# A two-layer hybrid backbone: attention values as one chain over all query blocks

## The chip, the core and the metric

The kernel runs on one core of a Trainium2 chip. The metric is the device time of one execution in microseconds (us), as the median of several runs. A core has five engines that each work through their own instructions in order and wait for one another by semaphores: PE (TensorE: matrix multiplications, and transposes as multiplications with an identity), DVE (VectorE), ACT (ScalarE), POOL (GpSimd) and SP, which here only issues DMAs.

## What is computed

Two layers over 1024 latent and 256 context tokens. Each layer projects a normalised and modulated stream into the inputs of three branches (windowed attention, a convolution with a LayerNorm, a bidirectional linear recurrence called LRU), gates and merges them, and normalises again. The change touches the values of attention, the two einsums with `p_loc` and `p_ctx`:

```python
def window_attention(q, k, v, k_ctx, v_ctx, sink):
    ...
    p = jax.nn.softmax(jnp.concatenate([s_loc, s_ctx, s_sink], -1), axis=-1)
    p_loc = p[..., :3 * BLOCK].astype(v.dtype)
    p_ctx = p[..., 3 * BLOCK:3 * BLOCK + C].astype(v.dtype)
    out = jnp.einsum('bnhgqj,bnjhd->bnqhgd', p_loc, vb) + jnp.einsum('bnhgqc,bchd->bnqhgd', p_ctx, v_ctx)
```

A query block is 128 queries of one key/value head with its four query heads. Its keys are two context blocks and up to three neighbouring latent blocks of 128: two to five key blocks. Layer 0 has 20 query blocks with 84 key blocks in all, layer 1 (latent queries only) 16 with 76.

## The kernel before

Every large product is made in single-precision parts: an operand is split into a rounded part on ACT (`whi`, `ph`, `hlhi`) and a remainder on DVE (`wlo`, `pl`, `hllo`), and the product is three (or, for the values, two) matmuls into one PSUM tile.

Each layer has two phases. In phase 1 nine generators run side by side: `lru`, `att_values`, `att_scores`, `lru_in`, `lru_out`, `att_proj`, `att_out`, `conv` and `gates`. A generator emits some instructions and yields the engine on which its next step waits. A `Driver` keeps a reckoning of each engine's time, picks by readiness and priority (`PRIO`) which generator goes on, and a scheduler behind it orders the instructions of each engine once more. So the order on an engine is fixed before the program runs, and every move of one generator moves the others. `gates` (24 weight columns with 2 or 3 products each) and the gating products of `lru_out`, `conv` and `att_out` are the reserve that fills PE while other generators wait.

Three pools are booked by counters: `sl` (10 wide SBUF slots), `hl_` (14 half slots of 128x512, for almost every generator) and `pl_` (4 PSUM tiles of one bank, shared by products, turned keys and value sums).

`att_values` takes one query block at a time. For each key block j it turns four 128x128 pieces of the probabilities into a PSUM tile `pt` (four transposes on PE), splits it into `ph` (ACT) and `pl` (DVE), and one step later lets the function `values` add two matmuls to the block's sum `yp`. After the last key block come its joining: `yt` (two copies on ACT, then two additions on DVE) and a DMA of the 128x512 result. Before each block it takes four half slots and one PSUM tile, and gives them back behind the joining. With T for the four transposes and V for the two matmuls, a block reads T0 T1 V0 T2 V1 ... V(last), joining.

The convolution's LayerNorm stands beside it: for a token tile, a sum matmul `ps<-sm` on PE, four centring instructions on DVE (`ab`, `acc2`, `acc`), four squares `sq` on ACT, a second sum matmul. It needs six half slots (`LH`). There are three such tiles in layer 0 and two in layer 1.

Of the kernel before, what the change touches and what calls it, by code (L numbers as in the profile page):

```python
# [9 lines left out]
F32R = mybir.dt.float32r  # L10
# [179 lines left out]
def kernel(  # L190
# [8 lines left out]
    pe, act, dve = Meter(nc.tensor, pe_cost), Meter(nc.scalar, act_cost), Meter(nc.vector, dve_cost)  # L199
# [19 lines left out]
    def f32(ap):  # L219
        return ap.bitcast(F32)  # L220

    def psum(n=512, name="ps"):
        return PM.tile([128, n], F32, tag="mm", name=name, bufs=4)
# [6 lines left out]
    ident = K.tile([128, 128], F32, tag="ident", name="ident")  # L230
# [121 lines left out]
    def split(src, hi, lo):  # L352
        act.activation(out=hi, in_=src, func=AF.Copy)
        dve.tensor_tensor(out=lo, in0=src, in1=f32(hi), op=ALU.subtract)
# [167 lines left out]
    def both(*conds):  # L522
        return lambda: all(c() for c in conds)

    def phase1(l, R, RH):
# [5 lines left out]
        sl, hl_, pl_ = Pool_(NS), Pool_(NHF), Pool_(4)  # L531
# [5 lines left out]
        def half(name, dt=F32):  # L537
            return RH.tile([128, 512], dt, tag="h", name=name, bufs=NHF)
# [323 lines left out]
        at = dict(proj=[], ready=[], done={0: 0, 1: 0}, issued=0, ks={}, vs={})  # L862
        tiles0 = 2 if last else 0
        blocks = [(kv, t) for kv in range(2) for t in range(tiles0, 10)]
# [159 lines left out]
                at["ready"].append((kv, tl, keys, pv, drv_.t["dve"]))  # L1024

        def att_values():
            for i in range(len(blocks)):
                yield ("pe", both(lambda: len(at["ready"]) > i, hl_.room(4)))
                kv, tl, keys, pv, tm = at["ready"][i]
                vs = at["vs"][kv]  # L1030
                hl_.take(4)
                yield ("pe", tm, lambda: pl_.used <= 2)
                pl_.take()
                yp = psum(name="yp")
                pend = None

                def values(j, ph, pl, stop):
                    pe.matmul(out=yp, lhsT=vs[:, keys[j], :], rhs=ph, start=(j == 0), stop=False)
                    pe.matmul(out=yp, lhsT=vs[:, keys[j], :], rhs=pl, start=False, stop=stop)

                for j in range(len(keys)):
                    pt = psum(name="pt")
                    for hh in range(4):
                        pe.transpose(pt[:, hh * 128:hh * 128 + 128], pv[hh][:, j * 128:j * 128 + 128], ident)
                    ph, pl = half("ph", F32R), half("pl", F32R)
                    split(pt, ph, pl)
                    yield "pe"
                    if pend:
                        values(*pend, False)
                        yield "pe"  # L1050
                    pend = (j, ph, pl)
                values(*pend, True)
                sl.give(2)
                yield "act"
                yt = half("yt")
                ypv = yp.rearrange("p (a e q) -> p a e q", e=2, q=128)
                ytv, yo = (yt[:, o:o + 256].rearrange("p (a q) -> p a q", q=128) for o in (0, 256))
                act.activation(out=ytv[0:64], in_=ypv[64:128, :, 0, :], func=AF.Copy)
                act.activation(out=ytv[64:128], in_=ypv[0:64, :, 1, :], func=AF.Copy)
                yield "dve"  # L1060
                for e in range(2):
                    r = slice(64 * e, 64 * e + 64)
                    dve.tensor_tensor(out=yo[r], in0=ypv[r, :, e, :], in1=ytv[r], op=ALU.add)
                sp.dma_start(out=ya_d[kv * 256:kv * 256 + 256, tl * 128:tl * 128 + 128].rearrange("(c p) t -> p c t", p=128),
                             in_=yo)
                pl_.give()
                hl_.give(4)
                at["done"][kv] += 1
                if at["done"][kv] == per_kv:
                    sl.give()  # L1070

        def att_out():
            for j in range(4):
                yield ("pe", lambda: at["done"][j // 2] == per_kv)

                def get(nt):
                    y = half("ya")
                    sp.dma_start(out=y[:, 0:nt[2]], in_=ya_d[j * 128:j * 128 + 128, nt[1]:nt[1] + nt[2]])
                    return y[:, 0:nt[2]]

                yield from gating(0, j, get, 1.0)
# [15 lines left out]
        def gates():  # L1097
# [27 lines left out]
            assert not todo  # L1125

        drv_.run([lru(), att_values(), att_scores(), lru_in(), lru_out(), att_proj(), att_out(), conv(), gates()], PRIO[l])
        assert wlive[0] == 0 and sl.used == 0 and hl_.used == 0 and pl_.used == 0

# [274 lines left out]
    for l in range(DEPTH):  # L1404
        drv_.phase = 2 * l
        phase1(l, RS, RH)
        ss.close()

        def open_b():
            hs.close()  # L1410
            return open_pool(f"b{l}", 1 - l)

        drv_.phase = 2 * l + 1
        phase2(l, lambda: open_pool(f"a{l}", l), open_b, lambda: open_pool(f"c{l}", l))
        if l < DEPTH - 1:
            hs, RH = open_pool(f"h{l + 1}", l)
            ss, RS = open_pool(f"s{l + 1}", 1 - l)
# [46 lines left out]
```

## Time and profile before

| | |
|---|---|
| median of 3 runs | 2307.63 us (2306.44 to 2307.89) |
| the profiled execution | 2307.8 us, span 2306.0 us |
| granted TensorE clock, mean | 0.99 |
| busy share of the span | PE 98%, weight loads 81%, DVE 73%, ACT 44% |

The span reaches from the first to the last instruction; 1.8 us lie outside it. Attention's values run in layer 0 from 460 to 925 us and in layer 1 from 1665 to 2062 us.

### The profile page before, as it was taken

The page shows a single profiled execution, that of the slowest core. Times are in us where ns is not written, and L with a number is a line of the kernel's source. Part 1 is how long each engine was busy: PE and PEld are TensorE (multiplying, and loading weights), DVE is VectorE, ACT ScalarE, POOL GpSimd, SP SyncE. Part 2 cuts the span into 40 slices and gives each one's busy share as a digit, 9 for nine tenths or more (in the row PEclk, how much of TensorE's full clock was granted, in tenths as well). Part 3 has the DMA queues.
Part 4 walks back from the last instruction along what each step waited for, and adds up shares of the span by engine and source line. Part 5 has one row for each costly group of instructions (what it writes and reads, how often), then busy time and mean ns, then how long its engine had stood idle before and what let it go on. Part 6 is the DMA issues. An engine that isn't in the chain of part 4 may idle for free.

```text
span 2306.0 us, 29961 instructions
## 1 busy us (share of the span) xinstructions
PE 2249.3 (98%) x11344; PEld 1871.8 (81%) x11344; DVE 1678.9 (73%) x2453; ACT 1003.4 (44%) x1642; POOL 86.7 (4%) x140
## 2 busy tenths in 40 slices
PE   7999999999999999999999999999999999999998
PEld 2888888888888887888888788888888878778886
DVE  5579967868959875545678749869778787655667
ACT  4555563245444575422122644565344456542110
POOL 1000000000000111000001100000000011000002
PEclk8999999999999999999999999999999999999999
DMA  7223323433334232655562222233423334347532
GB/s 276 76 73 101 115 73 126 142 112 108 108 101 138 80 117 87 203 167 168 151 206 74 94 66 67 80 92 128 142 90 97 89 122 131 111 136 227 160 128 92
DMA packets 270946, 279.90 MB, mean 121 GB/s; under 512 B 19769, under 2 KB 199889, under 8 KB 270801
## 3 DMA queue, kind: packets, MB, share of 16 engines
q1 hardware_dynamic: 242288, 226.06, 31.4%
q10 hardware_dynamic: 28512, 51.92, 6.4%
q8 instruction: 89, 1.46, 0.3%
q14 instruction: 57, 0.46, 0.1%
HBM read 203.04 MB, written 74.88 MB: 121 GB/s over the span
## 4 chain that ended last, share of the span: by engine, by line
PE 88%; DVE 5%; ACT 2%; DMA 2%; issue 2%; SPq 0%; POOLq 0%; POOL 0%; ACTq 0%; DVEq 0%
PE ps L73 82%; PE yp L73 3%; PE pt L73 2%; PE pa L73 1%; DVE acc L73 1%; DMA raw<-in_w_ada_dram 1%; DVE P L73 1%; DVE pl L73 1%; DVE wlo L73 1%; DMA yst<-yd 1%; ACT whi L73 0%; DMA qd<-qd 0%; DVE xp L73 0%; PE p L73 0%; ACT hf L73 0%
## 5 line engine op out<-in xcount | busy, mean ns | idle before, releaser
L73 PE MATMUL ps<-hlhi,whi 128*128 128x512 f32 x1728 | 681.9, 395 | 2.2 <-DVE gs L73 1.0
L73 PE MATMUL ps<-hllo,whi 128*128 128x512 f32 x1728 | 678.4, 393 | 0.0
L73 PE MATMUL ps<-hlhi,wlo 128*128 128x512 f32 x1728 | 676.8, 392 | 0.0
L73 PEld LDWEIGHTS ps<-hlhi,wlo 128*128 128x128 f32 x1728 | 325.8, 189 | 67.5 <-issue 0.4
L73 PEld LDWEIGHTS ps<-hlhi,whi 128*128 128x128 f32 x1728 | 326.5, 189 | 66.5 <-DVE pl L73 2.2
L73 PEld LDWEIGHTS ps<-hllo,whi 128*128 128x128 f32 x1728 | 326.2, 189 | 62.7 <-issue 0.7
L73 DVE SCALAR_TENSOR_TENSOR acc<-u,cwt,acc 128x1296 f32<-128x1296 f32 (+1 forms) x240 | 342.3, 1426 | 2.2
L73 ACT ACTIVATE whi<-raw 128x1024 fp32r<-128x1024 f32 x180 | 190.0, 1058 | 334.1 <-PE ps L73 299.9
L73 DVE TENSOR_TENSOR wlo<-raw,whi 128x1024 fp32r<-128x1024 f32 x180 | 220.4, 1225 | 95.1 <-ACT whi L73 91.5
L73 PE MATMUL ps<-yy,whi 128*128 128x512 f32 (+1 forms) x960 | 271.6, 368 | 2.8 <-DVE m L73 2.8
L73 PEld LDWEIGHTS ps<-yy,whi 128*128 128x128 f32 x960 | 173.7, 188 | 33.5 <-DVE m L73 3.2
L73 PE MATMUL ps<-yy,wlo 128*128 128x512 f32 (+1 forms) x480 | 176.6, 368 | 0.0
L73 ACT ACTIVATE ph<-pt 128x512 fp32r<-128x512 f32 x160 | 93.9, 591 | 130.5 <-PE pt L73 125.1
L73 DVE TENSOR_TENSOR pl<-pt,ph 128x512 fp32r<-128x512 f32 x160 | 108.9, 685 | 50.8 <-ACT ph L73 49.4
L73 PE MATMUL ps<-hchi,whi 128*128 128x256 f32 x480 | 135.6, 283 | 1.3 <-ACT whi L73 0.5
L73 ACT ACTIVATE P<-P,nm 128x640 f32<-128x640 f32 (+1 forms) x128 | 101.9, 798 | 79.7 <-DVE nm L73 79.6
L73 PE MATMUL ps<-hchi,wlo 128*128 128x256 f32 x480 | 135.3, 282 | 1.0 <-DVE wlo L73 1.0
L73 PE MATMUL ps<-hclo,whi 128*128 128x256 f32 x480 | 134.6, 281 | 0.0
L73 DVE CUSTOM_DVE_ANT_0 P<-ps,m_mid,nsink 128x640 f32<-128x640 f32 (+1 forms) x112 | 93.0, 859 | 42.3 <-PE ps L73 40.8
L73 ACT ACTIVATE tg<-ps,drv 128x512 f32<-128x512 f32 (+1 forms) x120 | 76.4, 637 | 68.3 <-PE ps L73 67.7
L73 PEld LDWEIGHTS ps<-yy,wlo 128*128 128x128 f32 x480 | 90.5, 188 | 15.0
L73 PE MATMUL pt<-ident,P 128*128 128x128 f32 x640 | 97.2, 274 | 3.1 <-DVE pl L73 1.4
(205 smaller groups left out, 3396.1 us busy)
## 6 DMA issues: line engine op xcount, KB each, us to landing
raw<-in_w_in_dram SPq DMA_DIRECT2D x60, 512.0 KB
raw<-in_w_ada_dram SPq DMA_DIRECT2D x48, 512.0 KB
raw<-in_w_gate_dram SPq DMA_DIRECT2D x48, 512.0 KB
th<-tg ACTq DMA_DIRECT2D x96, 256.0 KB
thl<-th SPq DMA_DIRECT2D x96, 256.0 KB
yd<-gs ACTq DMA_DIRECT2D x48, 256.0 KB
yst<-yd SPq DMA_DIRECT2D x48, 256.0 KB
raw<-in_w_branch_dram SPq DMA_DIRECT2D x24, 512.0 KB
```

The costliest lines, as they stand in the source:

```text
L73: return f(*a, **k)
```

## The change

`att_values` holds the pending key block in a list that outlives the query block. The turning of the next block's first key block is emitted ahead of the last `values` of the block before, and the joining comes behind that. When the next block's probabilities are not there yet, the pending step is flushed first. The PSUM tile for `yp` is taken at a block's first `values`, no longer ahead of its first turning. The four half slots are taken once, when the generator starts (that is at the start of phase 1), and given back at its end; each block takes one more for `yt`.

```diff
--- before.py
+++ after.py
@@ -1024,32 +1024,20 @@
                 at["ready"].append((kv, tl, keys, pv, drv_.t["dve"]))
 
         def att_values():
-            for i in range(len(blocks)):
-                yield ("pe", both(lambda: len(at["ready"]) > i, hl_.room(4)))
-                kv, tl, keys, pv, tm = at["ready"][i]
-                vs = at["vs"][kv]
-                hl_.take(4)
-                yield ("pe", tm, lambda: pl_.used <= 2)
-                pl_.take()
-                yp = psum(name="yp")
-                pend = None
-
-                def values(j, ph, pl, stop):
-                    pe.matmul(out=yp, lhsT=vs[:, keys[j], :], rhs=ph, start=(j == 0), stop=False)
-                    pe.matmul(out=yp, lhsT=vs[:, keys[j], :], rhs=pl, start=False, stop=stop)
-
-                for j in range(len(keys)):
-                    pt = psum(name="pt")
-                    for hh in range(4):
-                        pe.transpose(pt[:, hh * 128:hh * 128 + 128], pv[hh][:, j * 128:j * 128 + 128], ident)
-                    ph, pl = half("ph", F32R), half("pl", F32R)
-                    split(pt, ph, pl)
+
+            pend = []
+
+            def values():
+                q, j, ph, pl = pend.pop()
+                if j == 0:
+                    pl_.take()
+                    q["yp"] = psum(name="yp")
+                keys, yp, vs = q["keys"], q["yp"], at["vs"][q["kv"]]
+                pe.matmul(out=yp, lhsT=vs[:, keys[j], :], rhs=ph, start=(j == 0), stop=False)
+                pe.matmul(out=yp, lhsT=vs[:, keys[j], :], rhs=pl, start=False, stop=(j == len(keys) - 1))
+                if j < len(keys) - 1:
                     yield "pe"
-                    if pend:
-                        values(*pend, False)
-                        yield "pe"
-                    pend = (j, ph, pl)
-                values(*pend, True)
+                    return
                 sl.give(2)
                 yield "act"
                 yt = half("yt")
@@ -1061,13 +1049,36 @@
                 for e in range(2):
                     r = slice(64 * e, 64 * e + 64)
                     dve.tensor_tensor(out=yo[r], in0=ypv[r, :, e, :], in1=ytv[r], op=ALU.add)
+                kv, tl = q["kv"], q["tl"]
                 sp.dma_start(out=ya_d[kv * 256:kv * 256 + 256, tl * 128:tl * 128 + 128].rearrange("(c p) t -> p c t", p=128),
                              in_=yo)
                 pl_.give()
-                hl_.give(4)
+                hl_.give(1)
                 at["done"][kv] += 1
                 if at["done"][kv] == per_kv:
                     sl.give()
+
+            hl_.take(4)
+            for i in range(len(blocks)):
+                if pend and len(at["ready"]) <= i:
+                    yield from values()
+                yield ("pe", both(lambda: len(at["ready"]) > i, hl_.room()))
+                kv, tl, keys, pv, tm = at["ready"][i]
+                q = dict(kv=kv, tl=tl, keys=keys)
+                hl_.take(1)
+                yield ("pe", tm, lambda: pl_.used <= 2)
+                for j in range(len(keys)):
+                    pt = psum(name="pt")
+                    for hh in range(4):
+                        pe.transpose(pt[:, hh * 128:hh * 128 + 128], pv[hh][:, j * 128:j * 128 + 128], ident)
+                    ph, pl = half("ph", F32R), half("pl", F32R)
+                    split(pt, ph, pl)
+                    yield "pe"
+                    if pend:
+                        yield from values()
+                    pend.append((q, j, ph, pl))
+            yield from values()
+            hl_.give(4)
 
         def att_out():
             for j in range(4):
```

The number and the shapes of the instructions stay as they were. The order changes from the LRU stretch of layer 0 on, on every engine.

**The end of layer 1's attention, on PE and ACT.** In these rows `pt` are the turnings, `yp` the value sums, `ph` and `pl` the two parts, `P` the probabilities. On PE before, from the first turning of the last block but one (`pt_17719`) on:

```order
L73 MATMUL pt_17719<-ident_81,P_17307 128x128 x2
L73 MATMUL pt_17719<-ident_81,P_17349 128x128 x2
L73 MATMUL yp_17640<-pl_17694,vs_16094 128x512
L73 MATMUL pt_17728<-ident_81,P_17307 128x128 x2
L73 MATMUL pt_17728<-ident_81,P_17349 128x128 x2
L73 MATMUL yp_17640<-ph_17704,vs_16094 128x512
L73 MATMUL yp_17640<-pl_17705,vs_16094 128x512
L73 MATMUL yp_17718<-ph_17724,vs_16094 128x512
L73 MATMUL pt_17739<-ident_81,P_17307 128x128 x2
L73 MATMUL pt_17739<-ident_81,P_17349 128x128 x2
L73 MATMUL yp_17718<-pl_17725,vs_16094 128x512
```

After, the corresponding rows, from `pt_17710` on:

```order
L73 MATMUL pt_17710<-ident_81,P_17354 128x128 x2
L73 MATMUL pt_17710<-ident_81,P_17411 128x128 x2
L73 MATMUL yp_17674<-pl_17694,vs_16138 128x512
L73 MATMUL yp_17674<-ph_17704,vs_16138 128x512
L73 MATMUL pt_17727<-ident_81,P_17354 128x128 x2
L73 MATMUL pt_17727<-ident_81,P_17411 128x128 x2
L73 MATMUL yp_17674<-pl_17705,vs_16138 128x512
L73 MATMUL yp_17736<-ph_17715,vs_16138 128x512
L73 MATMUL yp_17736<-pl_17716,vs_16138 128x512
L73 MATMUL pt_17739<-ident_81,P_17354 128x128 x2
L73 MATMUL pt_17739<-ident_81,P_17411 128x128 x2
L73 MATMUL yp_17736<-ph_17732,vs_16138 128x512
```

Before, two turnings of the new block stand ahead of the old block's last `values` (`ph_17704`, `pl_17705`), and the new block's first `values` (`ph_17724`) follow at once; now one turning stands ahead of them, and a second is not far ahead. On ACT, in the same place, before:

```order
L73 ACTIVATE ph_17704<-pt_17699 128x512
L588 DMA yd13_136<-gs_17624 128x512
L73 ACTIVATE yt_17712<-yp_17640 64x256 x2
L73 ACTIVATE ph_17724<-pt_17719 128x512
L73 ACTIVATE ph_17733<-pt_17728 128x512
```

and after:

```order
L73 ACTIVATE ph_17704<-pt_17699 128x512
L73 ACTIVATE ph_17715<-pt_17710 128x512
L73 ACTIVATE yt_17721<-yp_17674 64x256 x2
L73 ACTIVATE ph_17732<-pt_17727 128x512
```

The copies `yt` of the old block's sum stood ahead of the new block's first `ph`; now that `ph` (`ph_17715`) stands ahead of them, and its second (`ph_17732`) behind.

**The second LayerNorm tile of layer 1, on PE and DVE.** On PE before, around the sum matmul `ps<-sm`; `ps<-hlhi,whi` and its like are a product of `gates` or of a gating:

```order
L73 MATMUL yp_16486<-ph_16629,vs_16094 128x512
L73 MATMUL yp_16486<-pl_16630,vs_16094 128x512
L73 MATMUL ps_16650<-sm_16618,ones_f_86 128x512
L73 MATMUL ps_16690<-hlhi_11640,whi_16473 128x512
L73 MATMUL ps_16690<-hllo_11641,whi_16473 128x512
L73 MATMUL ps_16690<-hlhi_11640,wlo_16474 128x512
L73 MATMUL ps_16690<-hlhi_11640,whi_16473 128x512
L73 MATMUL ps_16690<-hllo_11641,whi_16473 128x512
L73 MATMUL ps_16690<-hlhi_11640,wlo_16474 128x512
```

After, around the same sum matmul:

```order
L73 MATMUL pt_16606<-ident_81,P_16518 128x128 x2
L73 MATMUL ps_16631<-sm_16589,ones_f_86 128x512
L73 MATMUL pt_16606<-ident_81,P_16557 128x128 x2
L73 MATMUL pt_16639<-ident_81,P_16518 128x128 x2
L73 MATMUL pt_16639<-ident_81,P_16557 128x128 x2
L73 MATMUL yp_16671<-ph_16611,vs_16138 128x512
L73 MATMUL yp_16671<-pl_16612,vs_16138 128x512
L73 MATMUL yp_16671<-ph_16644,vs_16138 128x512
```

Before, at least six matmuls of a product follow the sum matmul; now turnings and `values` follow it directly. On DVE after, the centring and what stands behind it:

```order
L73 SCALAR_TENSOR_TENSOR ab_16491<-ps_16631,ab_16491 128x512 x2
L73 SCALAR_TENSOR_TENSOR acc2_16492<-ps_16631,acc2_16492 128x512
L73 SCALAR_TENSOR_TENSOR acc_15790<-ps_16631,acc_15790 128x512
L73 TENSOR_TENSOR pl_16612<-pt_16606,ph_16611 128x512
L73 SCALAR_TENSOR_TENSOR gs_16547<-gs_16547,ps_16550 128x512
L73 TENSOR_TENSOR gs_16547<-gs_16547,ya_16548 128x512
L73 TENSOR_TENSOR pl_16645<-pt_16639,ph_16644 128x512
```

The remainder `pl_16612`, which the second `yp` row above needs, stands behind four centring instructions that need the sum matmul.

## Rows read from the trace of the kernel before

**Rows 1.** The page's head and its busy times.

```profile
span 2306.0 us, 29961 instructions
...
PE 2249.3 (98%) x11344; PEld 1871.8 (81%) x11344; DVE 1678.9 (73%) x2453; ACT 1003.4 (44%) x1642; POOL 86.7 (4%) x140
```

**Rows 2.** Windows: length, busy PE, weight loads, DVE, ACT, POOL; PE clock, DMA.

```profile
190.00:335.00 145.00, 144.52 (x774) 121.35 (x773) 123.18 (x120) 74.72 (x101) 0.89 (x7) 1.00 0.31 101
460.00:925.00 465.00, 451.35 (x2532) 383.40 (x2533) 349.79 (x587) 239.70 (x470) 23.98 (x21) 0.99 0.34 106
925.00:1030.00 105.00, 104.67 (x555) 90.33 (x553) 51.20 (x78) 37.89 (x63) 0.30 (x3) 1.00 0.58 189
1660.00:2062.00 402.00, 391.20 (x1923) 324.90 (x1922) 304.75 (x502) 201.52 (x376) 17.14 (x16) 0.99 0.34 105
```

**Rows 3.** PE's idle time (us, times) at `yp`, then at `pt`, 460:925 us.

```profile
  ACT ph L73: 5.9, 6
  DVE pl L73: 2.8, 3
...
  DVE pl L73: 1.4, 1
  DVE yt L73: 0.5, 1
```

**Rows 4.** The same for layer 1, 1660:2065 us.

```profile
  ACT ph L73: 3.2, 3
  DVE yt L73: 0.8, 1
...
  ACT ph L73: 1.0, 1
```

**Rows 5.** Timeline of layer 1's end: start us, us, engine, tiles, [idle, releaser].

```profile
2045.07 0.40 PE L73 MATMUL yp<-pl,vs 128*128 128x512 f32 x1
2045.51 0.77 ACT L73 ACTIVATE yt<-yp 64x256 f32<-64x256 f32 x2 [1.66 <-PE yp L73]
2046.30 1.09 ACT L73 ACTIVATE ph<-pt 128x512 fp32r<-128x512 f32 x2
...
2046.95 0.50 PE L73 MATMUL yp<-ph,vs 128*128 128x512 f32 x1 [1.48 <-ACT ph L73]
...
2053.53 0.50 PE L73 MATMUL yp<-ph,vs 128*128 128x512 f32 x1 [1.48 <-ACT ph L73]
```

**Rows 6.** Chain that ended last, one turning: start us, us, what.

```profile
2048.68 0.44 PE pt L73 x4
```

**Rows 7.** Timeline around the third LayerNorm tile of layer 0.

```profile
904.97 0.39 PE L73 MATMUL ps<-hlhi,whi 128*128 128x512 f32 x1
...
905.20 0.39 PE L73 MATMUL ps<-hllo,whi 128*128 128x512 f32 x1
...
909.74 1.02 PE L73 MATMUL ps<-sm,ones_f 128*128 128x512 f32 x2
...
911.62 1.29 DVE L73 SCALAR_TENSOR_TENSOR ab<-ps,ab 128x512 f32<-128x512 f32 x2
...
912.83 1.28 DVE L73 SCALAR_TENSOR_TENSOR acc<-ps,acc 128x512 f32<-128x512 f32 x2
...
914.02 0.68 DVE L73 TENSOR_TENSOR pl<-pt,ph 128x512 fp32r<-128x512 f32 x1
...
914.76 0.79 PE L73 MATMUL yp<-ph,vs 128*128 128x512 f32 x1 [2.39 <-DVE pl L73]
```

**Rows 8.** Timeline of a wait inside a block, layer 0.

```profile
593.15 0.58 ACT L73 ACTIVATE ph<-pt 128x512 fp32r<-128x512 f32 x1
...
593.78 0.79 PE L73 MATMUL yp<-ph,vs 128*128 128x512 f32 x1 [2.29 <-ACT ph L73]
```

**Rows 9.** Windows of three stretches with a lower PE clock, layer 0.

```profile
593.50:597.00 3.50, 3.22 (x8) 2.54 (x9) 3.43 (x6) 1.20 (x4) 0.00 (x0) 0.51 0.51 148
791.50:798.30 6.80, 5.91 (x19) 4.73 (x18) 4.65 (x9) 4.59 (x10) 1.71 (x2) 0.50 0.11 41
914.40:917.80 3.40, 3.04 (x9) 2.56 (x10) 1.30 (x3) 2.60 (x6) 3.24 (x3) 0.50 0.21 77
```

## The prediction

> **What bounds the kernel now.** I read the page's busy times first, then windows by stage, then PE's idle time at the tiles of the values, and last the timeline at the places where that idle time stands. The page shows PE busy for 2249.3 of 2306.0 us [rows 1]: 57 us of idle time in all, at the start, at the change of phases and in the two stretches of attention. The windows give those stretches: PE is idle for 465 − 451.35 = 13.7 us in layer 0 and 402 − 391.20 = 10.8 us in layer 1, while DVE works for some 75% of both [rows 2]. Two matmuls of 512 columns that follow each other start 905.20 − 904.97 = 0.23 us apart, though each shows 0.39 us [rows 7]; they overlap, so a gap between them is lost, and a matmul's duration is not its price. With the same instructions on PE before and after, only gaps and the clock can change the time.
>
> Of those gaps the values own 5.9 + 2.8 at `yp` and 1.4 + 0.5 at `pt` in layer 0, 10.6 us [rows 3], and 3.2 + 0.8 + 1.0 = 5.0 us in layer 1 [rows 4]. Beside them stand three stretches of layer 0 with a granted clock of 0.50 to 0.51, the lower of the two levels (1.2 instead of 2.4 GHz): 3.5, 6.8 and 3.4 us [rows 9]. Each begins at a wait of the values: 2.29 us before 593.78 [rows 8], 1.4 us at `pt` for `pl` near 791 [rows 3], 2.39 us before 914.76 [rows 7]. At half the clock half of such a stretch is lost: 1.7, 3.4 and 1.7 us.
>
> The Trainium skill (Perfetto Trace Analysis, "Identifying the Most-Contended Engine") says that the busy share of matmuls is no good measure of how much room PE has, and that the busy share of weight loads should be read in its place. By that share, 81% here, some 430 us would be open to a better order. The starts 0.23 us apart say otherwise for this kernel: nothing but the 57 us is open, and I go by these.
>
> **What the change does, term by term.** A turning T takes 0.44 us [rows 6], a V two starts, 0.46 us.
>
> *1. Values inside a block, layer 0.* I counted, over the whole order on PE, the work that stands between a key block's last transpose and its first `yp` matmul. The split of `ph` on ACT alone lasts 0.58 us [rows 8]. In layer 0 the cover is under 0.75 us at 7 of 84 key blocks before, two of them at a LayerNorm (term 3); after, at 2, one at a LayerNorm. In layer 1 it is none of 76 before and 6 after: four at a LayerNorm, one at the bare end (term 2), one alone. So outside terms 2 and 3: five before, two after. The five pay, with the small waits of the layer, 10.6 less what stands at LayerNorms (2.39, 1.4 and 0.5) = 6.3 us, and 1.7 us of clock: 8.0. For two I leave 2.6, somewhat less than two fifths of it, since one of the two is the very first key block, where two waited before. Term: −5.4, between −8.0 (both hidden) and −2.0 (they cost nearly what five did).
>
> *2. The bare end of layer 1.* There no product is left and PE has only T and V. Before, `ph` of a new block stands behind both `yt` copies, and those behind the old block's last V: the last `yp` starts at 2045.07, `yt` at 2045.51, `ph` at 2046.30, the next `yp` at 2046.95 [rows 5]. From start to start 1.88 us, of which its own 0.23 is work: 1.65 lost, twice (the second before 2053.53), 3.3 in all. After, the new block's first `ph` is ahead of `yt`, but its second is behind. The same 1.88 us now have 0.23 of the old V, 0.46 of the first new V and 0.44 of a turning as cover: 0.75 lost, at three boundaries, 2.3. Term: −1.0. If ACT gets round to it sooner it is −3.3; if DVE's additions, which stand ahead of `pl`, come last, +1.0.
>
> *3. LayerNorm next to the values.* In rows 7 the sum matmul starts at 909.74; the DVE's centring follows (911.62, 912.83), then `pl`, and the first V comes at 914.76, with 2.39 us of idle time. The order has such a place, where after the sum matmul no run of product matmuls covers the centring, twice before (both in layer 0) and four times after: the first two tiles of layer 0 and both of layer 1. Layer 0's third tile, bare before, has a product behind it now. Price before: 1.4 + 3.4 at the first, 0.5 + 2.39 + 1.7 at the third, and the 1.0 us at layer 1's first tile [rows 3, 4, 7, 9]: 10.4. A place costs 1.0 to 4.8. One of the new four has its `pl` covered by six matmuls, one has the half-size context tile, and the two in layer 1 look like rows 7; I take 3.4 on average, 13.6. Term: +3.2, between 4 × 1.0 − 10.4 = −6.4 and 4 × 4.8 − 10.4 = +8.8.
>
> *4. PSUM tiles.* A new `ps`, `pt` or `yp` must wait until the tile that held its buffer is read. `yp` is taken later, which frees one for a while, but joining and turning overlap more. In the two attention stretches, the LRU stretch of layer 0 and the one of layer 1 the places with under 2 us of PE work between are 35 before and 54 after. The two attention stretches have 24.5 us of idle time, the values 15.6 of it; the other 8.9 over 35 places is 0.25 a place. Term: between 0 and 19 × 0.25 = +4.8; most of them are covered anyway, I take +2.
>
> *5. Four half slots held from the start.* `gates` needs one, `att_proj` up to six, `lru_in` three, of what is now ten. In the order five gate products of layer 0 leave the LRU stretch for later (35 tiles in the wide buffers before, 31 after; in layer 0 18 and 13). Each is up to 24 matmuls, 5.4 us of cover, 27 in all. At 190:335 us PE is busy for 144.5 of 145 us and DVE for 123.2 [rows 2]. Without the 27 us PE has 118 us of work against DVE's 123: at most 5 us in which PE stands, if DVE never does, and they would not come back, for later (925:1030) DVE has only 51 of 105 us. Part of the projections moves into the stretch. Term: 0 to +5, I take +1.
>
> The sixth edit, flushing the pending step when the next block isn't ready, only restores the old order there: nothing. The moved DMA `ya` has work behind it until `att_out` reads it a whole head later; but for the last block, where layer 1's last product hides it as before: nothing.
>
> Sum: −5.4 − 1.0 + 3.2 + 2 + 1 = −0.2 us, against the profiled execution's own 2307.8 us (span 2306.0 and 1.8 around it): 2307.6. The median of the runs is 2307.63, 0.2 below that execution: 2307.5 us.
>
> **Rivals.**
> *A, faster.* The chain helps everywhere and the LayerNorm places are hidden: term 1 at −8.0 and two of the four places of term 3 free (6.8 − 10.4 = −3.6), the rest as above: −9.6, 2298 us. For it: five short covers become two, and the longest gaps of layer 0 go. Against: four bare LayerNorm places in the order.
> *B, slower, at the LayerNorm.* Centring ahead of `pl` on DVE costs at each of the four places what it cost at 791 and 914, 4.8 us with the lower clock: term 3 at +8.8 and the sum at +5.4, 2313 us. It decides from 4.5 us a place on. For it: the DVE rows of layer 1's second tile are those of rows 7. Against: a clock stretch need not follow each gap; the two of 1.48 us in rows 5 have none.
> *C, slower, for want of buffers.* The Trainium skill (same page, "Optimization Strategy") holds that gaps that repeat on the engine that ought to be full can mean too few buffers for the next tile; holding four half slots for good goes that way. As a mechanism here it is term 5 at its upper end, +5, and one more stretch of the lower clock (3.4 lost): −0.2 + 4 + 3.4 = +7.2, 2315 us. Against it: PE's idle time in that stretch is 0.5 us now [rows 2].
> *D, no effect.* The order before already places two turnings ahead of the old block's last V at the end of layer 1; if that holds in most places the chain adds nothing, and terms 3 to 5 at small values leave 2307 to 2311. It falls together with no change.
>
> **How the numbers follow.** A measurement of this kernel tells no change from one of 0.2%, 4.6 us. My forecast, with D, has 0.40: the terms cancel within that. A has 0.28, B 0.20, C 0.12. So faster 0.28, same 0.40, slower 0.32. All lower bounds together make −17.7 and all upper ones +17.6; not all come at once, and some two thirds, 2296 to 2319, leave out about 2 in 10. The forecast's own range is 2303 to 2312.
>
> **What would show it.** Term 1: PE's idle time at `yp` and `pt` in layer 0's attention under 7 us. Term 2: the gaps at the last blocks near 0.75 us, with `yt` between two `ph` of the new block. Term 3: gaps of 1 to 3 us at `yp` right behind `ps<-sm`, in layer 1 most of all, with DVE's `ab` and `acc` ahead of `pl`, and stretches of clock 0.5 behind them; none at layer 0's third tile. Term 4: more waits of `ps` and `pt` for evacuations. Term 5: idle PE between 190 and 335 us. I'd be wrong if the lower clock took more than 10 us in the attention stretches, or if PE stood at places that hold no values at all.

## The result: slower, and outside the range

After the change the median is 2340.31 us (2339.93 to 2342.58); the kernel before, on the same chip, 2307.76 us (2306.44 to 2308.19). The ratio is 1.0144, with an interval of 1.0129 to 1.0159: 32.5 us slower. The forecast of no change was wrong, and so was the size of every rival: the time went the way of B and C, with four to six times what they added.

### The profile page after: what moved, and what is told of

Read it like the earlier page. It is cut to its first block, busy times and chain, and to the rows that moved or that the text cites. A ratio compares the mean times of both kernels' runs of the same rounds, so it can differ in the third digit from the quotient of the medians.

```text
span 2338.3 us, 29949 instructions
## 1 busy us (share of the span) xinstructions
PE 2259.6 (97%) x11344; PEld 1875.1 (80%) x11344; DVE 1679.1 (72%) x2453; ACT 1007.8 (43%) x1642; POOL 86.8 (4%) x140
## 4 chain that ended last, share of the span: by engine, by line
PE 85%; DVE 8%; ACT 3%; issue 2%; DMA 2%; SPq 0%; POOL 0%; POOLq 0%; DVEq 0%; ACTq 0%
PE ps L73 78%; DVE acc L73 3%; PE yp L73 2%; PE pt L73 2%; PE pa L73 1%; DVE P L73 1%; DVE wlo L73 1%; DVE pl L73 1%; DMA qd<-qd 1%; ACT P L73 1%; ACT whi L73 0%; PE p L73 0%; DVE xp L73 0%; ACT hf L73 0%; ACT ph L73 0%
## 5 line engine op out<-in xcount | busy, mean ns | idle before, releaser
L73 PEld LDWEIGHTS pt<-ident,P 128*128 128x128 f32 x640 | 80.2, 143 | 36.3 <-ACT P L73 5.1
```

The costliest lines, as they stand in the source:

```text
L73: return f(*a, **k)
```

## The profile after

The page's head and busy times of the changed kernel:

```profile
span 2338.3 us, 29949 instructions
...
PE 2259.6 (97%) x11344; PEld 1875.1 (80%) x11344; DVE 1679.1 (72%) x2453; ACT 1007.8 (43%) x1642; POOL 86.8 (4%) x140
```

The instructions on PE are as many as in [rows 1]. PE's idle time rises from 56.7 to 2338.3 − 2259.6 = 78.7 us, and 10.3 us more are "busy": matmuls at the lower clock, and the first ones behind a gap. DVE works as long as before to 0.2 us, so nothing was added; it moved.

Windows of the changed kernel (length, busy PE, weight loads, DVE, ACT, POOL; PE clock, DMA): the LRU stretch, attention of layer 0, what follows it, attention of layer 1, and two stretches of the lower clock:

```profile
190.00:335.00 145.00, 138.01 (x731) 117.61 (x730) 127.65 (x121) 77.24 (x99) 0.90 (x7) 0.98 0.27 88
452.00:888.00 436.00, 418.99 (x2374) 353.84 (x2373) 335.39 (x571) 232.94 (x456) 14.82 (x16) 0.99 0.34 105
888.00:1010.00 122.00, 122.00 (x637) 104.52 (x636) 44.55 (x58) 40.80 (x65) 8.65 (x8) 1.00 0.45 144
1697.00:2095.00 398.00, 379.29 (x1837) 310.75 (x1837) 297.12 (x480) 193.66 (x362) 18.25 (x16) 0.99 0.33 103
252.60:259.40 6.80, 4.35 (x12) 3.25 (x13) 6.76 (x5) 2.80 (x4) 0.00 (x0) 0.50 0.06 19
1908.10:1911.50 3.40, 3.27 (x9) 2.13 (x10) 2.71 (x7) 1.16 (x2) 0.08 (x1) 0.50 0.40 140
```

Beside [rows 2]: PE idles 7.0 us of the LRU stretch (0.5 before) and starts 43 matmuls fewer in it; attention idles 17.0 us in layer 0 (13.7) and 18.7 us in layer 1 (10.8).

Idle time alone hides the clock, so I add up **lost time**: for each PE instruction the time to the next one's start, less the median of that time for instructions of its kind (same tiles, same shape). Waits and lower clock are both in it. It is worked out from all PE records of a trace, and the kernels of the experiments stand beside it:

| lost, us | before | after | e1 | e2 | e5 | e7 | e16 | e17 | e18 |
|---|---|---|---|---|---|---|---|---|---|
| LRU stretch, 60 us to the first `yp` | 7.1 | 20.9 | 7.1 | 20.7 | 7.1 | 7.0 | 7.2 | 7.0 | 7.0 |
| attention, layer 0 | 26.7 | 31.1 | 56.0 | 20.9 | 38.2 | 33.9 | 32.8 | 30.9 | 27.0 |
| between the two | 12.8 | 12.7 | 14.4 | 12.0 | 14.1 | 15.9 | 15.3 | 14.8 | 11.4 |
| attention, layer 1 | 20.0 | 33.7 | 26.4 | 36.8 | 32.3 | 22.1 | 30.7 | 36.2 | 32.6 |

Before to after: +13.8, +4.4, −0.1, +13.7, together 31.8 of the span's 32.3 us.

**The LRU stretch.** Waits of PE in the changed kernel, 190 to 452 us (us in total, times, longest):

```profile
PE ps L73 <- ACT xh L73: 6.1, 1, 6.1
PE ps L73 <- DVE pl L73: 2.7, 1, 2.7
PE pt L73 <- ACT P L73: 2.4, 1, 2.4
PE ps L73 <- ACT whi L73: 1.9, 1, 1.9
```

The first is 6.1 us in one piece. Its timeline (start, us, engine, tiles, [idle, releaser]):

```profile
248.48 0.28 PE L73 MATMUL ps<-hchi,wlo 128*128 128x256 f32 x1
248.72 1.55 DVE L73 SCALAR_TENSOR_TENSOR xc<-X,prm,xc 128x1284 f32<-128x1284 f32 x1
250.18 1.56 DVE L73 SCALAR_TENSOR_TENSOR acc<-u,cwt,acc 128x1296 f32<-128x1296 f32 x1
...
252.00 1.55 DVE L73 SCALAR_TENSOR_TENSOR xc<-X,prm,xc 128x1284 f32<-128x1284 f32 x1
253.46 1.56 DVE L73 SCALAR_TENSOR_TENSOR acc<-u,cwt,acc 128x1296 f32<-128x1296 f32 x1
253.58 1.27 ACT L73 ACTIVATE xh<-xc 128x1284 fp32r<-128x1284 f32 x1 [9.94 <-DVE xc L73]
254.91 1.44 PE L73 MATMUL ps<-xh,lwh 128*128 128x260 f32 x3 [6.14 <-ACT xh L73]
```

PE's last product ends at 248.8. The LRU matmul needs `xh`, a split of `xc`, whose taps are 1.55 us each on DVE and alternate there with the convolution's taps `acc`. PE has nothing else, and the clock falls to half from 252.6 to 259.4 us; PE works for 4.35 us of these (window 252.60:259.40). Before, PE waited nowhere for `xh` in this stretch: gate products stood there. ACT's reading of the tiles that gate products leave (`tg<-ps`) counts them; from 190 to 335 us, before and then after:

```profile
L73 ACT ACTIVATE tg<-ps,drv x7: 450/678/693, 224.6 to 326.4; 128x512 f32<-128x512 f32 x4, 128x256 f32<-128x256 f32 x3
L73 ACT ACTIVATE tg<-ps,drv x3: 467/687/691, 223.6 to 241.5; 128x512 f32<-128x512 f32 x2, 128x256 f32<-128x256 f32 x1
```

Four of seven tiles are gone, and the last of the three is read before the wait begins. In the runs below there are three in e2, which holds the slots, and seven in e1, e3, e5 and e6, which take them late or have enough.

**Attention, layer 0.** PE's waits in the changed kernel, 452 to 888 us:

```profile
PE ps L73 <- DVE pl L73: 4.1, 6, 1.5
PE yp L73 <- ACT ph L73: 3.7, 5, 1.6
PE pt L73 <- ACT tg L73: 3.0, 2, 2.2
PE pt L73 <- DVE ada L73: 1.9, 1, 1.9
PE ps L73 <- DVE gs L73: 0.9, 1, 0.9
PE ps L73 <- ACT tg L73: 0.8, 1, 0.8
PE yp L73 <- ACT tg L73: 0.8, 1, 0.8
PE pt L73 <- DVE yt L73: 0.7, 1, 0.7
```

A `yp` that waits for `ph` waits for its operand. A `ps` released by `pl` or `nm`, or a `pt` by `tg`, `ada`, `yt` or `rstd` (the LayerNorm's root), reads none of them: there PE waits for a PSUM tile to be emptied. I sort PE's waits in the two attention stretches so (releasers are inferred, so a few tenths may stand in the wrong column); the first number is layer 0, the second layer 1:

| us, layer 0 / layer 1 | `yp` for its own `ph`, `pl` | `pt` for probabilities `P` | for a tile's reader |
|---|---|---|---|
| before | 8.7 / 3.6 | 0 / 0 | 2.6 / 4.6 |
| after | 3.7 / 7.0 | 0 / 1.7 | 12.5 / 6.6 |
| e1 | 3.5 / 6.1 | 11.8 / 0 | 13.3 / 2.0 |
| e5 | 4.9 / 9.9 | 7.8 / 0 | 4.7 / 3.2 |
| e7 | 11.7 / 3.2 | 0 / 0 | 4.4 / 6.3 |
| e16 | 4.7 / 3.4 | 1.5 / 3.6 | 8.4 / 3.5 |
| e17 | 3.6 / 4.9 | 1.5 / 3.8 | 6.7 / 5.7 |
| e18 | 7.8 / 7.2 | 0 / 1.7 | 2.6 / 6.0 |

**The second LayerNorm tile of layer 1**, the one whose order is shown ahead of the prediction, in the timeline of the changed kernel:

```profile
1956.72 1.02 PE L73 MATMUL ps<-sm,ones_f 128*128 128x512 f32 x2
1957.58 0.38 PE L73 MATMUL pt<-ident,P 128*128 128x128 f32 x2
1957.78 1.29 DVE L73 SCALAR_TENSOR_TENSOR ab<-ps,ab 128x512 f32<-128x512 f32 x2 [0.80 <-PE ps L73]
1958.00 0.60 ACT L73 ACTIVATE ph<-pt 128x512 fp32r<-128x512 f32 x1 [1.61 <-PE pt L73]
...
1958.99 1.28 DVE L73 SCALAR_TENSOR_TENSOR acc<-ps,acc 128x512 f32<-128x512 f32 x2
...
1960.18 0.68 DVE L73 TENSOR_TENSOR pl<-pt,ph 128x512 fp32r<-128x512 f32 x1
...
1960.92 0.66 PE L73 MATMUL pt<-ident,P 128*128 128x128 f32 x4 [2.96 <-DVE pl L73]
```

The centring stands ahead of `pl` as forecast, and it costs 2.96 us, but not at `yp`: the next turning waits for the PSUM tile that `pl` has yet to read.

**The bare end of layer 1**, the waits of `yp` at the last three boundaries, with the copies `yt` ahead of the first. There the new block's first `yp` waits, at the other two its second:

```profile
2073.77 0.77 ACT L73 ACTIVATE yt<-yp 64x256 f32<-64x256 f32 x2
...
2075.21 0.50 PE L73 MATMUL yp<-ph,vs 128*128 128x512 f32 x1 [1.45 <-ACT ph L73]
...
2081.63 0.49 PE L73 MATMUL yp<-ph,vs 128*128 128x512 f32 x1 [0.26 <-ACT ph L73]
...
2087.31 0.50 PE L73 MATMUL yp<-ph,vs 128*128 128x512 f32 x1 [0.50 <-ACT ph L73]
```

## The experiments

The theories, by the letters that some expectations use. **S**: the four half slots held from the start of the phase cost. **J**: the joined chain itself costs; its later form, **P**, is that the next block's first turning stands on PE ahead of probabilities that aren't scaled yet. **L**: the LayerNorm places cost (rival B). **O**: neither; any edit shuffles the order, and that of before happens to be a good one. A neutral edit is one that none of S, J and L gives a cause to cost: another number of the planner, more slots, a hold at the LayerNorm. "Over before" is the difference to the kernel before as it ran on the same chip beside the experiment (its medians there are 2309.35 to 2311.05).

### S against J: the two halves of the change apart

*e1, the chain with the slots taken late* (edit of the changed kernel; the `take(4)` at the start goes):

```diff
-                yield ("pe", both(lambda: len(at["ready"]) > i, hl_.room()))
+                yield ("pe", both(lambda: len(at["ready"]) > i, hl_.room(1 if i else 5)))
...
-                hl_.take(1)
+                hl_.take(1 if i else 5)
```

Expected: 

> The change, but its four half slots are taken when the first query block is ready instead of at the start of phase 1. Theory S (the held slots starve the other generators): the 6.1 us wait of the LRU products for xh near 255 us is gone and with it 8 to 15 of the 32 us, 2325 to 2332. Theory J (the joined chain itself makes waits in attention): 2330 to 2335, only the LRU stretch (8 us) is saved. Theory O (the order of before is a tuned one, and any order that differs this much loses): anywhere from 2312 to 2345, with waits at other places than in the change.

Measured: 2348.34 us, ratio 1.0160 (1.0143 to 1.0177), 38.2 over before.

*e2, the slots without the chain* (edit of the kernel before):

```diff
         def att_values():
+            hl_.take(4)
             for i in range(len(blocks)):
-                yield ("pe", both(lambda: len(at["ready"]) > i, hl_.room(4)))
+                yield ("pe", lambda: len(at["ready"]) > i)
...
-                hl_.take(4)
...
-                hl_.give(4)
+                if i == len(blocks) - 1:
+                    hl_.give(4)
```

Expected: 

> The kernel before with only the four half slots held from the start of phase 1 to the end of attention, blocks one at a time as before. Theory S: slower by half of the 32 us or more, over 2323, with the wait of the LRU products near 255 us. Theory J: 2308 to 2316 (at most the 8 us of the LRU stretch). Theory O: 2312 to 2335.

Measured: 2337.98 us, ratio 1.0111 (1.0096 to 1.0126), 27.8 over before.

*e3, the chain with the slots given back at each flush* (edit of the changed kernel: `hl_.give(4)` behind the flush, and `need = 1 if pend else 5` for room and take).

Expected: 

> The change, but the four half slots are taken when a chain starts and given back when it is flushed (seven or so times a kernel), none held ahead of attention. Theory S: close to before, 2304 to 2314. Theory J: 2325 to 2340. Theory O: anywhere from 2312 to 2340.

Measured: 2354.10 us, ratio 1.0183 (1.0168 to 1.0198), 43.9 over before.

Each half costs by itself, and they don't add. No theory had e1 or e3 inside its range; e2 came where S put it. The table of lost time tells them apart by place. The LRU stretch loses 20.7 us with the slots alone (e2), with the same 6.1 us at `xh`, and 7.1 with the chain alone (e1; 7.0 in e3): that stretch is S. But e1 loses 56.0 us in layer 0's attention instead (e3 as much, and in layer 1 35.9 on top, so that handing back was no help). Its timeline there:

```profile
692.98 0.49 PE L73 MATMUL yp<-pl,vs 128*128 128x512 f32 x1 [0.79 <-DVE pl L73]
...
695.58 1.56 DVE L73 SCALAR_TENSOR_TENSOR acc<-u,cwt,acc 128x1296 f32<-128x1296 f32 x1
...
697.06 0.15 DVE L73 TENSOR_TENSOR es<-nm,sink 128x4 f32<-128x4 f32 x1
697.17 1.57 DVE L73 SCALAR_TENSOR_TENSOR acc<-u,cwt,acc 128x1296 f32<-128x1296 f32 x1
...
698.66 0.15 DVE L73 TENSOR_TENSOR es<-es,sm 128x4 f32<-128x4 f32 x1
698.78 1.57 DVE L73 SCALAR_TENSOR_TENSOR acc<-u,cwt,acc 128x1296 f32<-128x1296 f32 x1
700.26 0.17 DVE L73 RECIPROCAL es<-es 128x4 f32<-128x4 f32 x1
...
700.47 0.51 ACT L73 ACTIVATE P<-P,es 128x256 f32<-128x256 f32 x1 [3.02 <-DVE es L73]
701.03 0.48 PE L73 MATMUL pt<-ident,P 128*128 128x128 f32 x1 [7.55 <-ACT P L73]
```

The first turning of the joined block stands on PE and waits 7.55 us for the last scaling of `P`, whose three small DVE steps (0.15 to 0.17 us) each come behind a tap of 1.56 or 1.57 us. In the kernel before, unjoined, no `pt` waits for `P`.

### S: enough slots for all

With `NHF` 18 in place of 14 the held four leave as many as before the change. Edit of each: `NS, NHF, ... = 10, 18, ...`.

*e5, the changed kernel with 18.* Expected: 

> The change with 18 half slots instead of 14, so that the four held ones stand on top of what the other generators had before. Theory S (held slots): the LRU stretch goes back from 20.9 to 7 us lost, and the whole to 2308 to 2320. Theory O (luck of the order): LRU stretch back too, for its order there is that of before again, but attention lost anywhere, 2315 to 2350. Theory J (the joined chain): attention of layer 0 loses 45 us or more as in the run that took the slots late, 2335 to 2350.

Measured: 2332.74 us, ratio 1.0102 (1.0087 to 1.0117), 23.4 over before.

*e6, e2 with 18.* Expected: 

> The kernel before, with four half slots held from the start (as in the run that held them alone), and 18 instead of 14: nobody else is short of slots, blocks are not joined. Theories S and J: 2303 to 2313. Theory O: 2312 to 2335.

Measured: 2319.74 us, ratio 1.0046 (1.0031 to 1.0061), 10.4 over before.

*e7, the kernel before with 18.* Expected: 

> The kernel before with 18 half slots, nothing else. Theory S in its plain form (more slots, more cover): 2298 to 2308. Theory O: the order differs from that of before only where 14 slots did bind; 2305 to 2325. A run well under 2307 would be a better version.

Measured: 2322.62 us, ratio 1.0057 (1.0042 to 1.0072), 13.3 over before.

Holding costs nothing when there are enough (e6 is 2.9 us under e7), and the LRU stretch is back at 7.1 us in all three. The chain still costs 10.1 us over e7. And more slots, which only give the planner more freedom, cost the kernel before 13.3 us: that is O (with another number of the planner they cost 1.9 us, e15 against e12 below).

### O: how far a neutral edit moves the time

*e4, the kernel before with another number of the planner*, `LAG_CONV` (22, 11) for (20, 10). Expected: 

> The kernel before with one number of the planner moved by a tenth (LAG_CONV 22 and 11 for 20 and 10), the values as they were. Theories S and J: no cause to change, 2305 to 2311. Theory O: 2312 to 2330, for every order after the first LayerNorm tile is another one.

Measured: 2317.83 us, ratio 1.0029 (1.0018 to 1.0039), 7.6 over before.

*e8, the changed kernel with the same.* Expected: 

> The change with the planner's LAG_CONV moved by a tenth (22 and 11 for 20 and 10), as was done to the kernel before. Theory S: the LRU stretch still loses 21 us and the whole is 2333 to 2348. Theory O: 2318 to 2360, with attention's share moving by 10 us or more either way.

Measured: 2338.57 us, ratio 1.0129 (1.0112 to 1.0146), 29.2 over before.

*e12, the kernel before with `LAG_Q` (3.5, 1.0) for (3.0, 0.5).* Expected: 

> A second control of the luck of the order: the kernel before with LAG_Q 3.5 and 1.0 for 3.0 and 0.5, nothing else. S, J and L: no cause for a change, 2305 to 2312. O: 2312 to 2335.

Measured: 2306.26 us, ratio 0.9978 (0.9967 to 0.9989), 4.4 under before, the fastest kernel of the study.

*e13, the changed kernel with the same.* Expected: 

> The changed kernel with LAG_Q (3.5, 1.0) for (3.0, 0.5), the edit that moved the kernel before to 2306.3 us. Changed less unchanged was +32.5 us as the kernels stand, +20.8 with the other LAG_CONV and +22.8 with the hold at the LayerNorm. If only the LRU stretch is a cost of the change and all else is the luck of an order: 2306 + 14 = 2320 us, between 2314 and 2325. If the joined chain costs some 10 us of its own beside it: 2330 us, between 2326 and 2340. PE's lost time in the LRU stretch is near 21 us in both cases.

Measured: 2348.67 us, ratio 1.0163 (1.0146 to 1.0180), 37.6 over before. *The same edit with 18 slots, changed (e14) and unchanged (e15):*

Expected of e14: 

> The changed kernel with 18 half slots and the same LAG_Q. The LRU stretch loses 7 us as before the change. Against the kernel before with 18 half slots and the same LAG_Q (run beside it): if the chain itself costs something, 8 to 14 us more, as 2332.7 against 2322.6 without the LAG_Q edit; if that was luck, between -5 and +5 us.

Expected of e15: 

> The kernel before with 18 half slots and LAG_Q (3.5, 1.0): the partner of the run above, no theory of the change speaks of it alone. Edits of this kind moved the kernel before by -5 to +13 us, so 2302 to 2323 us.

Measured: e14 2335.46 us, ratio 1.0106 (1.0090 to 1.0122), 24.4 over before; e15 2308.53 us, ratio 0.9989 (0.9979 to 0.9998), 2.5 under.

Changed less unchanged, each as its distance to before: 32.5 as they stand, 29.2 − 7.6 = 21.6 with the `LAG_CONV` edit, 37.6 + 4.4 = 42.0 with the `LAG_Q` edit; with 18 slots 10.1 and 24.4 + 2.5 = 26.9. The sign never turns and the size goes from 10.1 to 42.0. O alone is refuted; so is any account that explains single microseconds of the 32.5. The kernel before moved by −4.4 (e12), +4.2 (e11, below), +7.6 (e4) and +13.3 us (e7) under neutral edits, and from e7 to e15 by 13.3 + 2.5 = 15.8 us: a single difference of less than that shows nothing by itself. e13, and e14 against e15, came out above every range given for them; their waits, under P below, say where, not why.

### L: values held back at a LayerNorm

A flag `ln` is set at a tile's first sum matmul and cleared with the last centring; `att_values` yields `("pe", lambda: not state["ln"])` where it yielded `"pe"`, so that products fill the place.

*e9, in the changed kernel.* Expected: 

> The change, with the values' turnings and matmuls held back while a LayerNorm tile stands between its first sum matmul and its last centring, so that products cover it. If the LayerNorm places are the larger part of what attention lost (theory L: some 12 us of idle time and 8 us of lower clock at four of five tiles), 2318 to 2328, with the LRU stretch still at 21 us lost and layer 1's attention back near 20 to 24 from 33.7. If attention lost by the general luck of the order (O), layer 1's share stays over 28 and the whole at 2333 to 2350.

Measured: 2337.75 us, ratio 1.0115 (1.0100 to 1.0131), 27.1 over before.

*e10, with 18 slots.* Expected: 

> The same hold, with 18 half slots, so that neither the held slots nor the LayerNorm places are left of the change. Theory S and L together: 2308 to 2322, no longer slower than the kernels with 18 slots and no chain (2320 to 2323). Theory J (the joined chain makes waits wherever it stands): 2328 to 2336. O: anywhere from 2312.

Measured: 2329.46 us, ratio 1.0077 (1.0062 to 1.0092), 18.8 over before.

*e11, in the kernel before.* Expected: 

> The same hold in the kernel before, blocks one at a time, 14 slots. Theory L: layer 0's two LayerNorm places, which cost some 10 us with their lower clock, shrink: 2298 to 2306, a version better than both. O: the order of before is a tuned one, and the hold reorders the rest: 2310 to 2330.

Measured: 2314.92 us, ratio 1.0021 (1.0011 to 1.0031), 4.2 over before.

The hold does its work at the second tiles: within 7 us behind the sum matmul of layer 0's and of layer 1's second tile PE's gaps fall from 2.76 and 2.96 us to none in e9. It gives 32.5 − 27.1 = 5.4 us and 23.4 − 18.8 = 4.6 us, no more than a neutral edit may; changed less unchanged with the hold in both is 27.1 − 4.2 = 22.9 us. L is at most a part, not the cause. At layer 1's first tile the 2.1 us before the sum matmul stay in e9 (4.4 in e10): there the sum itself waits for POOL's `sm`, behind the convolution's last tap on DVE, which no centring explains.

### P: joining only what is ready

*e16, e5 with a stricter rule* (a block is joined only when its probabilities have been ready for 4 us in the planner's reckoning):

```diff
-                if pend and len(at["ready"]) <= i:
+                if pend and (len(at["ready"]) <= i or at["ready"][i][4] + 4.0 > drv_.t["pe"]):
```

Expected: 

> The changed kernel with 18 half slots, and a block joined to the one before only when its probabilities have been ready for 4 us in the planner's reckoning; else the pending step is flushed first. If the chain costs because the first turning of a block stands on PE ahead of probabilities that aren't scaled yet: the wait of 7.5 us at pt for P is gone, its lower clock (1.7) too, 2332.7 - 7.5 - 1.7 = 2323.5 us, between 2319 and 2327. If the joining itself, wherever it stands, is what costs (PSUM, LayerNorm): 2330 us or more.

Measured: 2326.20 us, ratio 1.0066 (1.0051 to 1.0081), 15.2 over before.

*e17, e1 with the same line.* Expected: 

> The changed kernel without the early hold (as the run with the four half slots taken at the first ready block, 2348.3 us), and a block joined only when its probabilities have been ready for 4 us in the planner's reckoning. If the chain costs because a block's first turning stands on PE ahead of probabilities not yet scaled: the two waits of 11.8 us at pt in layer 0 and a lower clock behind them (3.4 us at half speed, so 1.7, once or twice) go: 2348.3 - 11.8 - 2.5 = 2334 us, between 2329 and 2338. If the joining costs wherever it stands: 2342 us or more.

Measured: 2331.14 us, ratio 1.0089 (1.0070 to 1.0108), 20.1 over before.

Both came as P expects: 8.2 us less than e5, which a neutral edit may do too, and 18.1 less than e1, beyond any neutral edit seen here. In layer 0 the waits of `pt` for `P` go from 7.8 to 1.5 and from 11.8 to 1.5 us; lost time there from 38.2 to 32.8 and from 56.0 to 30.9. e16 stands 1.9 us over e7, which has no chain at all. In the orders of e1 and e5 the chain's cost in layer 0 is mainly this wait. In other orders it is not: in layer 0 the changed kernel, e13 and e14 wait for no `P` at all, and yet e13 loses 37.0 us there against 24.5 in its partner e12, and e14 38.7 against 25.4 in e15. In e14 the waits for a tile's reader are 15.0 us against 4.6, in e13 8.5 against 5.2. So P is shown for e1 and e5, and isn't the cause of the 32.5. In layer 1 the rule gained nothing (32.3 to 30.7, 26.4 to 36.2): there `P` waits of 3.6 and 3.8 us came up.

### Layer 1 alone

*e18: layer 0 has the `att_values` of before, layer 1 that of the change.* Expected: 

> Layer 0 has the attention values of the kernel before, layer 1 those of the changed one, with its four half slots held from the start of layer 1's first phase. Layer 0 is then that of before, to the instruction. If what layer 1's attention lost (+13.7 us of PE's time) is the change's own, from the chain and the held slots there: 2307.8 + 13.7 = 2321 us, between 2316 and 2327. If it came from what layer 0 had left over for later: 2308 us, between 2303 and 2313. In layer 1 the waits of ps on POOL's sm and of yp at the LayerNorm tiles (3.9 us each in the changed kernel) should stand again in the first case.

Measured: 2323.76 us, ratio 1.0051 (1.0036 to 1.0066), 12.8 over before. PE's waits in layer 1's attention in e18, 1660 to 2100 us:

```profile
PE yp L73 <- ACT ph L73: 5.1, 7, 1.5
PE pt L73 <- DVE pl L73: 3.0, 1, 3.0
PE ps L73 <- POOL sm L812: 2.1, 1, 2.1
PE yp L73 <- DVE pl L73: 2.0, 1, 2.0
PE pt L73 <- ACT P L73: 1.7, 2, 0.9
PE pt L73 <- DVE yt L73: 1.5, 2, 1.0
```

These are the waits of the changed kernel there, one by one (7.0 us of `yp` for its own parts, `P` 1.7, `sm` 2.1, `pt` for `pl` 3.0), though layer 0 is that of before (PE's instructions come in the order of before until 1483 us). Layer 1's 13 us are made in layer 1. Whether by the slots or by the chain stays open: the slots alone lose there too (e2, 36.8 us, with a wait of 5.6 us for `P`), the chain with enough slots as well (e5, 32.3, against 22.1 in e7), and the chain with late slots less (e1, 26.4 against 20.0 before).

## Why the prediction was wrong, point by point

Of the 32.5 us the LRU stretch holds 13.8, attention of layer 1 13.7 and attention of layer 0 4.4. The first part is shown by experiment; of the second it is shown that it is made in layer 1, not which half of the change makes it; the third is less than neutral edits make. The sizes under the terms don't add up to the whole: the waits of 2.19 us at layer 0's second LayerNorm tile and of 2.96 at layer 1's count in term 3 and in term 4.

**Term 5, the held slots: the step that failed.** I took +1 and bounded it by 5 us. Measured: +13.8 us, in the changed kernel as in e2, and nothing where the slots are late or enough. The mechanism was seen (gate products leave the stretch; rival C), but its bound compared sums: 118 us of PE's work against 123 us of DVE's, "at most 5 us in which PE stands, if DVE never does". A sum is no schedule. PE stands when the one result that it needs is late, and `xc` is late since its taps alternate with another generator's on a DVE that is 88% busy (127.65 of 145 us). With no gate product at hand PE stood for 6.14 us, worked at half the clock for 4.35 us at its end and behind it (some 2.2 lost), and stood for 1.9, 2.4 and 2.7 us later.

**Term 4, PSUM tiles.** I took +2, at most 4.8, from 0.25 us a place. Waits for a tile's reader grew by 9.9 us in layer 0 and 2.0 in layer 1. The price of a place was averaged over places that had cover; at the longer waits the reader itself stands behind other work, as `pl` behind the centring at 1960.18 above. Unjoined kernels have 2.3 to 6.2 us of such waits in layer 0 (before, e2, e4, e6, e7, e11, e12, e15), joined ones 4.7 to 15.0; under the same edit the joined kernel always has more, but with 18 slots only 4.7 against 4.4 (e5, e7). That the chain makes them is read from the waits of many kernels; no run took PSUM tiles away or added them.

**Term 1, layer 0's values.** Nearly right: away from the LayerNorm places `yp`'s waits for its own parts fall from 6.3 to 3.3 us, and the low-clock stretch behind 593.78 (1.7 lost) is gone: −4.7, where −5.4 stood. My sign of it, idle time at `yp` and `pt` under 7 us, was wrong: it is 10.4, since 5.9 us of it now stands at `pt`, nearly all for tiles.

**Term 2, the bare end.** The sum is right, by luck in part: 1.45 + 0.26 + 0.50 = 2.2 us, 2.3 forecast. The first is twice the forecast, for there `yt` still stands ahead of the new block's first `ph` on ACT, as before the change; at the other two it stands ahead of the second, as forecast, and they are shorter than forecast.

**Term 3, LayerNorm.** I took +3.2, at most +8.8. Counted as in the prediction, gaps within 7 us behind the sum matmul and half of each low-clock stretch, the places cost before 2.04 + 2.94 us of gaps and 5.1 of clock, 10.1; after 2.76 (layer 0's second), 3.93 and 3.88 (layer 1) and 8.5 of clock, 19.1. That is +9.0, the upper bound and rival B's price. None at layer 0's third tile, as forecast. But 2.10 of it, the wait for `sm`, and 0.92, a wait for `P` at layer 1's second tile, stand ahead of the sum matmuls, where no centring can make them; without these it is +6.0. And e9 gives back no more than some 5 us when values keep away. One sign of being wrong that I had named, more than 10 us of the lower clock in the attention stretches, could tell nothing: I had left out a stretch in layer 1 (1972.50:1979.30 at 0.50), and with it the kernel before has 20.5 us, the changed one 17.1. The other came: 6.14 us at `xh`, a place that holds no values.

**What no term had.** The joined chain puts the next block's turning on PE ahead of other work, and of the unjoined kernels only e2 waits there for `P` at all. The sixth edit (flush when not ready) I costed at nothing, as it "only restores the old order"; but "ready" there means that the scaling has been emitted and is due by the planner's reckoning, not that it has run: in e1 its small DVE steps stood behind taps. In the changed kernel itself this wait is small (1.7 us in layer 1, and 2.4 at the first block, inside the LRU stretch); with slots to spare it is 7.8 us (e5), with late ones 11.8 (e1). So the two halves of the change don't add: 27.8 us for the slots, 38.2 for the chain, 32.5 for both. A possible reason is that the gate products which the held slots keep out of the LRU stretch cover waits later; no run tried that by itself.

**The rivals.** C named the right place and the right shortage for 13.8 of the 32.5 us and priced them at 8.4 (5, and 3.4 of clock). The Trainium skill's rule beside it (Perfetto Trace Analysis, "Optimization Strategy": repeated gaps can mean too few buffers) agrees with e5 and e6, where 18 half slots bring the LRU stretch from 20.9 and 20.7 to 7.1 us, and does not hold for the whole kernel, which more slots made 13.3 us slower before the change. By the share of weight loads, one of the two measures that the Trainium skill (Perfetto Trace Analysis, "Identifying the Most-Contended Engine") names for TensorE, nothing happened: 81% before, 80% after, while PE's idle time told of 22 of the 32 us. A is out: the gain of term 1 came without the −8.0 that A put on it, and was outweighed by terms 3 to 5. Of D nothing is left.

## What to carry to other kernels

A reservation made early is paid by whoever shares the pool: before adding one, look for the stretch in which the reserve work of the other users is the only cover, and price it by the longest chain behind a shared engine, not by sums of work. A step that is put ahead on a full engine must be ready by the clock of the engine that makes its operand; "emitted" is not "done". And where a planner sets the order, run the same neutral edits on both kernels before believing a difference of under 15 us or so.

## What the runs showed of the hardware

In the changed kernel the granted clock was 0.50, the lower of the two levels, from 252.6 to 259.4 us, over the end of the wait of 6.14 us, and from 1908.1 to 1911.5, behind waits of 2.02 and 2.10 us. At 0.50 matmuls of 512 columns start 0.43 us apart (257.09, 257.52, 257.94), at 1.00 0.23 us (259.44, 259.68, 259.90), so half of PE's working time in such a stretch is lost: some 2.2 us of the 4.35 in the first, 1.6 of the 3.27 in the second. Not every wait is followed by one: behind those of 2.40 and 2.75 us that end at 438.76 and 445.44 the clock stayed at 1.00, and behind the one of 2.29 us in the kernel before [rows 8] it was 0.51 [rows 9]. By these runs the length of a single wait does not tell its price in clock. On DVE a step of 0.15 us cost PE some 1.5 us three times over in e1, for each stood behind a tap: with instructions of ten times its length in the queue, a short step's price is its place.
